# A float32 transformer trunk of split matmuls: the first blocks of x split straight from PSUM, and two column sets of the FFN's first projection taking turns

## The chip, the cores and the metric

The kernel runs on one core of a Trainium2 chip. The metric is the device time of one execution in microseconds; the times given are medians over runs of the same program. One profiled execution gives the trace.

## What is computed

The reference is a trunk of two layers on x (512 tokens by 1024 channels, float32). Each layer is an FFN, a token mixer (pooling, differential attention, a gated recurrence) and a second FFN, each with a norm ahead and a residual behind; a last norm ends it. The change touches the four FFNs only, whose first projection is this:

```
def swiglu(h, w_in, w_out):
    gate, up = jnp.split(h @ w_in, 2, axis=-1)
    return (jax.nn.silu(gate) * up) @ w_out
```

Here h is the normed x (512 x 1024) and w_in is 1024 x 5632, so gate and up have 2816 columns each.

## The kernel before

**Split matmuls.** Float32 values are split into a high and a low part (`wh` and `wl` of a weight block, `zh` and `zl` of the activations). One product is three matmuls: high by high, high by low, low by high. ScalarE makes the high part by a copy (`split_hi`), VectorE the low one by a subtraction (`low`, inside `split_hi`). A helper records every operation of the engines, so that nearly all rows have line 83, and operations are told apart by the names of their tiles.

**Seven products.** `seven()` computes a 2 x 2 block product by a scheme with seven block products, P1, P2, Q5, Q3, P6, P7, Q4, in this order. Their left operands are blocks of the transposed and gained x or sums of them: A11, A12, S1 (= A21 - A22), S4 (= A12 - S2), S2, S3, A22. Their right operands are sums of weight blocks, and these sums are not made by an engine: a block `raw` is loaded by SP's DMA queue (L368), used, and then changed in place by an accumulating DMA that GpSimd issues (L371) once the low part has been taken. The block b1 serves P1, Q5, P6 and Q4 in turn, b2 serves Q3 and P7. Each product has two units, n0 and n1, with a block of 256 rows each; a unit is 12 matmuls.

**Order of the work.** `ffn()` (L462) cuts the 2816 columns into six sets, `quad(j)` (L467): four of 512 columns and two of 384. Each set is 14 units, in the list `units`. The main loop runs a unit's matmuls and then `gap()`, which evicts what the unit completed and issues splits up to three units ahead:

```
for i in done:
    flush()
    ...
    u.after()
...
lows = splits_to(done[-1] + 3)
side.run()
```

Evictions are ScalarE copies (P1, Q5) and chains on VectorE: c (P2), v (Q3), and for P6 and P7 `u`, then `v` or `q5`; P6's six operations work on two row tiles. `defer(n, fn)` puts work n gaps later; `side` holds small work on parameters that runs in gaps with room. Loads are issued as far ahead as the number of blocks held (`held`, per set) allows. All blocks, high and low parts and most activations come from one pool of 43 tiles of 128 x 1024; PSUM has eight banks.

**The start.** `prologue` (L1271) loads parameters, constants and x on SP's queue, warms TensorE with matmuls on zeros, transposes a block of x into PSUM (`zt`), copies it to SBUF with the norm's gain (`zf`, ScalarE, four pieces of 256 columns), and splits it (`z_hilo`: `zh` by ScalarE, `zl` by VectorE, 1024 columns each). The four blocks of x follow each other (`z_block`), their sums for S1, S2, S3, S4 are made on VectorE (`zs`) and split, `squares` gathers the norm's sums of squares of x, and `derived_steps` computes parameters that the mixer needs, the first of them from a softplus of the recurrence's parameters (tiles `m`).

Of the kernel before, what the change touches and what calls it, by code (L numbers as in the profile page):

```python
# [9 lines left out]
F32R = mybir.dt.float32r  # L10
AF = mybir.ActivationFunctionType
ALU = mybir.AluOpType
ADD, SUB, MUL, MAX, MIN = ALU.add, ALU.subtract, ALU.mult, ALU.max, ALU.min
# [93 lines left out]
def trunk_kernel(ctx, tc, xn, pm, fin, cst, bd, f1i, f1o, win, wbp, wba, wbl, wout, f2i, f2o, out):  # L107
    nc = tc.nc
    V, A, PE, SP = Counted(nc.vector, 0.075, 0.00104), Counted(nc.scalar, 0.14, 0.00083), Counted(nc.tensor, 0.0, 0.00042), nc.sync
# [11 lines left out]
    def big(dt=F32, name="b"):  # L121
        return bp.tile([128, 2 * S], dt, tag="b", name=name)
# [8 lines left out]
    def bank(name="ps"):  # L131
        return pp.tile([128, S], F32, tag="ps", name=name)
# [4 lines left out]
    def f(t):  # L137
        return t.bitcast(F32)
# [3 lines left out]
    def flush():  # L142
        for fn in later:
            fn()
        later.clear()
# [13 lines left out]
    par = cp_.tile([128, NPAR], F32, tag="par", name="par")  # L159
# [18 lines left out]
    x = {}  # L178
    st = {"r": {}}
    units = []  # L180
# [7 lines left out]
    def defer(n, fn):  # L188

        tasks.setdefault(clock["gap"] + n, []).append(fn)  # L190
# [76 lines left out]
    def z_hilo(name):  # L267
        src = take(name)
        hi, lo = big(F32R, "zh"), big(F32R, "zl")
        A.activation(out=hi, in_=src, func=AF.Copy)  # L270
        later.append(lambda: V.tensor_tensor(out=lo, in0=src, in1=f(hi), op=SUB))
        zc[name] = (hi, lo)

    def z_sum(name, a, b, op):
        a, b = take(a), take(b)
        t = zf[name] = big(name="zs")
        V.tensor_tensor(out=t, in0=a, in1=b, op=op)

    def z_ready(role, n, got):

        got.add(role)
        if role == "A11":
            defer(n, lambda: z_hilo("A11"))
        if role in ("A21", "A22") and {"A21", "A22"} <= got:
            defer(n, lambda: (z_sum("S1", "A21", "A22", SUB), z_hilo("S1")))
            defer(n + 5, lambda: z_hilo("A22"))
        if role != "A12" and {"A11", "A21", "A22"} <= got:
            defer(n + 1, lambda: z_sum("S2", "S1", "A11", SUB))
            defer(n + 3, lambda: z_hilo("S2"))
            defer(n + 4, lambda: (z_sum("S3", "A11", "A21", SUB), z_hilo("S3")))  # L290
        if role == "A12":
            defer(n, lambda: z_hilo("A12"))
            defer(n + 1, lambda: (z_sum("S4", "A12", "S2", ADD), z_hilo("S4")))
            got.clear()
# [169 lines left out]
    def ffn(wi, wo, done, order0, rf, lim0=12):  # L464
        H = {}

        def quad(j, order, fresh):  # L467
            c0, w = ((0, 512), (16, 384), (4, 512), (19, 384), (8, 512), (12, 512))[j]
            u, c11, q5, v, th0, th1 = {}, {}, {}, {}, {}, {}
            held = {}  # L470

# [16 lines left out]
            def copies(dst):  # L488
                def fn(ps):
                    dst.update(enumerate(two("u")))  # L490
                    for tt in range(2):
                        A.activation(out=dst[tt][:, 0:w], in_=ps[tt][:, 0:w], func=AF.Copy)
                return fn
# [87 lines left out]
            def wap(r, c, k0, k1):  # L581
# [1 line left out]
                return wi[512 - r * 512 + k0 * 128:512 - r * 512 + k1 * 128, o:o + w].rearrange("(k p) f -> p k f", p=128)  # L583

            seven(order, 4, w, lambda name, k: [a[:, k * 256:k * 256 + 256] for a in zc[name]], wap,
                  {"P1": p1, "P2": p2, "Q5": copies(q5), "Q3": q3, "P6": p6, "P7": p7, "Q4": q4}, (lim0, 12, 10, 8, 8, 8)[j], fresh=fresh)

        n0 = len(units)
        later_order = ["P1", "P2", "Q5", "Q3", "P6", "P7", "Q4"]
        for j in range(6):  # L590
            quad(j, order0 if j == 0 else later_order, j == 0 and order0[1] == "Q5")
        nz = len(units) - 1
        add_hook(nz, zc.clear)

# [674 lines left out]


    def prologue(gain):  # L1271
        SP.dma_start(out=par, in_=pm)
        SP.dma_start(out=cs[:, 0:256], in_=cst[:, 0:256])
        warm = slot(F32R, "warm")
        V.memset(f(warm), 0.0)
        wps = bank("warm")

        def warming(n):
            for _ in range(n):
                PE.matmul(wps, lhsT=warm[:, 0:128], rhs=warm, start=True, stop=True)  # L1280

        warming(14)
        n = 0
        blocks_ = [(0, 1), (0, 0), (1, 0), (1, 1)]
        for hh, kk in blocks_:
            for tt in range(2):
                t = 2 * hh + tt
                x[t, kk] = slot(name="x")
                SP.dma_start(out=x[t, kk], in_=xn[t * 128:t * 128 + 128, kk * S:(kk + 1) * S])
            n = min(n + 2, 4)  # L1290
            loads(n)
        SP.dma_start(out=cs[:, 256:NCST], in_=cst[:, 256:NCST])
        roles = [role_of(hh, kk, 0) for hh, kk in blocks_]
        zb = [z_block(hh, kk, role, gain) for (hh, kk), role in zip(blocks_, roles)]
        zb[0]()
        warming(8)
        z_hilo("A11")
        flush()
        for fn in splits_to(0):
            fn()  # L1300
        zb[1]()
        lows = splits_to(1)
        z_hilo("A12")
        for fn in lows:
            fn()
        flush()
        for fn in splits_to(2):
            fn()
        defer(0, zb[2])
        defer(1, zb[3])  # L1310
        got = {"A11"}
        z_ready(roles[2], 1, got)
        z_ready(roles[3], 2, got)
        defer(4, lambda: (z_sum("S4", "A12", "S2", ADD), z_hilo("S4")))
        for i in range(4):
            defer(2 + i, lambda i=i: squares(i // 2, i % 2))
        side.gap += 1
        side.add("derived", derived_steps())

    def derived_steps():  # L1320
        def halves():
# [89 lines left out]
            state["dma"] += 1  # L1411
            state["held"] += len(b.loads)

    def split_hi(i):
        u = units[i]
        if not u.block:
            return lambda: None
        u.hi, u.lo = big(F32R, "wh"), big(F32R, "wl")
        todo = []
        for n, view, o, shape in u.pieces:  # L1420
            src = view(u.block.raw[n])
            size = math.prod(shape)
            cut = lambda t: t[:, o:o + size] if len(shape) == 1 else t[:, o:o + size].rearrange("p (k f) -> p k f", f=shape[-1])
            hi, lo = cut(u.hi), cut(u.lo)
            A.activation(out=hi, in_=src, func=AF.Copy)
            todo.append((lo, src, f(hi)))

        def low():
            for lo, src, hi in todo:
                V.tensor_tensor(out=lo, in0=src, in1=hi, op=SUB)  # L1430
            todo.clear()
            if u.acc:
                u.acc(u.block.raw[0])
            elif last_use[id(u.block)] == i:
                state["held"] -= len(u.block.raw)
                u.block.raw = None
            loads()
        return low

    def splits_to(i):  # L1440
        lows = []
        while state["split"] < len(units) and state["split"] <= i:
            lows.append(split_hi(state["split"]))
            state["split"] += 1
        return lows

# [131 lines left out]
```

## Time and profile before

| what | value |
|---|---|
| median of 3 runs | 2153.4 us (2152.71 to 2156.05) |
| profiled execution, its own time | 2148.72 us |
| its span | 2147.0 us |
| TensorE (PE) busy | 2086.4 us, 97% of the span |
| VectorE (DVE) busy | 1658.0 us, 77% |
| ScalarE (ACT) busy | 1192.8 us, 56% |
| data moved | 314.61 MB, mean 147 GB/s |

The busy times are shares of the whole span, which has stages of different kinds: the FFNs' first and second projections and the mixers. The four first projections are at the beginning of each FFN; the first starts the program. A wait in brackets behind a row is the idle time of that engine just before it, with the one that ended it. Matmul rows overlap: the distance between the starts of two of them is what one costs.

### The profile page before, as it was taken

The page shows a single profiled execution, that of the slowest core. Times are in us where ns is not written, and L with a number is a line of the kernel's source. Part 1 is how long each engine was busy: PE and PEld are TensorE (multiplying, and loading weights), DVE is VectorE, ACT ScalarE, POOL GpSimd, SP SyncE. Part 2 cuts the span into 40 slices and gives each one's busy share as a digit, 9 for nine tenths or more (in the row PEclk, how much of TensorE's full clock was granted, in tenths as well). Part 3 has the DMA queues.
Part 4 walks back from the last instruction along what each step waited for, and adds up shares of the span by engine and source line. Part 5 has one row for each costly group of instructions (what it writes and reads, how often), then busy time and mean ns, then how long its engine had stood idle before and what let it go on. Part 6 is the DMA issues. An engine that isn't in the chain of part 4 may idle for free. (4 is left out here: it accounts for less than half of the span.)

```text
span 2147.0 us, 26106 instructions
## 1 busy us (share of the span) xinstructions
PE 2086.4 (97%) x9648; PEld 1735.6 (81%) x9648; DVE 1658.0 (77%) x2355; ACT 1192.8 (56%) x1763; POOL 343.4 (16%) x292
## 2 busy tenths in 40 slices
PE   7999999999999999999999999999999999999998
PEld 5888888788787878987878988877887877888786
DVE  5877898598677487779977778976967766877797
ACT  6554565646563554546665555565455536555564
POOL 1222230000000022322312222300000000222230
PEclk9999999999999999999999999999999999999999
DMA  8888896122225278898967889941221353888894
GB/s 224 181 153 191 196 200 180 50 79 88 67 81 172 78 141 169 165 200 206 207 162 142 170 179 232 185 127 60 79 79 59 116 154 84 175 151 193 203 177 106
DMA packets 194096, 314.61 MB, mean 147 GB/s; under 512 B 10544, under 2 KB 86832, under 8 KB 193968
## 3 DMA queue, kind: packets, MB, share of 16 engines
q0 software_dynamic: 76288, 138.43, 38.9%
q1 hardware_dynamic: 117680, 174.51, 24.9%
q8 instruction: 75, 1.23, 0.2%
q14 instruction: 53, 0.43, 0.1%
HBM read 310.80 MB, written 2.10 MB: 146 GB/s over the span
## 5 line engine op out<-in xcount | busy, mean ns | idle before, releaser
L83 DVE TENSOR_TENSOR wl<-raw,wh 128x1024 fp32r<-128x1024 f32 (+2 forms) x696 | 709.1, 1038 | 204.6 <-ACT wh L83 202.4
L83 ACT ACTIVATE wh<-raw 128x1024 fp32r<-128x1024 f32 (+2 forms) x696 | 610.5, 906 | 264.5 <-DMA raw<-in_f1i_dram 115.4
L83 PE MATMUL ps<-z,wh 128*128 128x512 f32 x1216 | 380.1, 393 | 0.0
L371 POOL DMA_DIRECT2D raw<-in_f2i_dram x96 | 115.9, 1223 | 1133.5 <-DVE wl L83 390.1
L83 PE MATMUL P<-wl,zh 128*128 128x512 f32 (+1 forms) x768 | 287.5, 374 | 8.3 <-DVE wl L83 8.3
L83 PE MATMUL P<-wh,zh 128*128 128x512 f32 (+1 forms) x768 | 286.9, 374 | 2.1 <-ACT wh L83 2.1
L83 PE MATMUL P<-wh,zl 128*128 128x512 f32 (+1 forms) x768 | 285.9, 372 | 0.0
L83 PEld LDWEIGHTS ps<-z,wh 128*128 128x128 f32 x1216 | 227.1, 188 | 51.0 <-issue 3.4
L83 PE MATMUL ps<-z,wl 128*128 128x512 f32 x608 | 237.0, 390 | 0.0
L83 PE MATMUL Q<-wl,zh 128*128 128x512 f32 (+1 forms) x576 | 218.5, 379 | 14.5 <-DVE wl L83 14.5
L83 PE MATMUL Q<-wh,zh 128*128 128x512 f32 (+1 forms) x576 | 221.0, 384 | 7.5 <-ACT zh L83 3.9
L83 PE MATMUL Q<-wh,zl 128*128 128x512 f32 (+1 forms) x576 | 217.1, 377 | 5.4 <-DVE zl L83 5.4
L371 POOL DMA_DIRECT2D raw<-in_f1i_dram x96 | 116.0, 1232 | 377.8 <-DVE wl L83 276.5
L83 PEld LDWEIGHTS P<-wl,zh 128*128 128x128 f32 x768 | 144.5, 188 | 33.7 <-DVE wl L83 14.0
L83 PEld LDWEIGHTS P<-wh,zh 128*128 128x128 f32 x768 | 144.5, 188 | 24.3 <-ACT wh L83 4.4
L83 PEld LDWEIGHTS P<-wh,zl 128*128 128x128 f32 x768 | 144.6, 188 | 19.6
L83 PE MATMUL P<-wl,ah 128*128 128x512 f32 x352 | 138.2, 393 | 3.3 <-DVE wl L83 3.1
L83 PEld LDWEIGHTS Q<-wl,zh 128*128 128x128 f32 x576 | 109.6, 190 | 37.1 <-DVE wl L83 22.9
L83 PE MATMUL P<-wh,ah 128*128 128x512 f32 x352 | 137.4, 390 | 0.0
L83 PE MATMUL P<-wh,al 128*128 128x512 f32 x352 | 137.2, 390 | 0.0
L83 PEld LDWEIGHTS ps<-z,wl 128*128 128x128 f32 x608 | 114.1, 188 | 23.7
L83 PEld LDWEIGHTS Q<-wh,zh 128*128 128x128 f32 x576 | 109.8, 191 | 25.1 <-ACT zh L83 5.6
(189 smaller groups left out, 3412.2 us busy)
## 6 DMA issues: line engine op xcount, KB each, us to landing
raw<-in_win_dram SPq DMA_DIRECT2D x84, 512.0 KB, 4.3
raw<-in_f1i_dram POOLq DMA_DIRECT2D x64, 512.0 KB, 7.2
raw<-in_f2i_dram POOLq DMA_DIRECT2D x64, 512.0 KB, 6.9
raw<-in_f2i_dram SPq DMA_DIRECT2D x52, 512.0 KB, 5.1
raw<-in_f1i_dram SPq DMA_DIRECT2D x50, 512.0 KB, 5.8
raw<-in_f1o_dram POOLq DMA_DIRECT2D x40, 512.0 KB, 8.0
raw<-in_f2o_dram POOLq DMA_DIRECT2D x40, 512.0 KB, 8.2
raw<-in_f1o_dram SPq DMA_DIRECT2D x30, 512.0 KB, 7.3
```

Source lines behind the costliest of these rows:

```text
L83: return fn(*args, **kw)
L371: return lambda raw: GP.dma_start(out=raw[:, 0:n * w].rearrange("p (k f) -> p k f", f=w), in_=src, accum_op=ADD)
```

## The change

It has two parts, both in the order of work; what is multiplied with what stays the same.

In `ffn()`, the set (19,384) changes places with (4,512), so that both sets of 384 columns come second and third, and the 28 units of these two are put in turn: P1 of the one (two units), P1 of the other, P2 of the one, and so on. The number of blocks that may be held follows the sets.

```
-            c0, w = ((0, 512), (16, 384), (4, 512), (19, 384), (8, 512), (12, 512))[j]
+            c0, w = ((0, 512), (16, 384), (19, 384), (4, 512), (8, 512), (12, 512))[j]
...
-                  ..., (lim0, 12, 10, 8, 8, 8)[j], fresh=fresh)
+                  ..., (lim0, 12, 12, 10, 8, 8)[j], fresh=fresh)
...
         for j in range(6):
             quad(j, order0 if j == 0 else later_order, j == 0 and order0[1] == "Q5")
+            if j == 2:
+                n1 = len(units) - 28
+                units[n1:] = [units[n1 + 14 * s + 2 * p + n] for p in range(7) for s in range(2) for n in range(2)]
```

In `prologue`, the transfers of parameters and constants go to ScalarE's queue. A new `direct(b)` splits the blocks A11 and A12 of x straight from PSUM: ScalarE makes zh and VectorE zl, in four pieces each; the full copy zf, which the sums need, is made by ScalarE later (`full`). The first weight block's high part is made by VectorE, between the first and the second piece of zl. Eight warming matmuls behind the first transposes become six, the sums are deferred by fewer gaps, the squares by others, and the derived parameters by 30 gaps.

```
     def prologue(gain):
-        SP.dma_start(out=par, in_=pm)
-        SP.dma_start(out=cs[:, 0:256], in_=cst[:, 0:256])
...
+        nc.scalar.dma_start(out=cs[:, 0:256], in_=cst[:, 0:256])
+        nc.scalar.dma_start(out=par, in_=pm)
...
-        zb[0]()
-        warming(8)
-        z_hilo("A11")
-        flush()
-        for fn in splits_to(0):
-            fn()
-        zb[1]()
-        lows = splits_to(1)
-        z_hilo("A12")
...
+        def direct(b, mid=lambda: None):
+            (hh, kk), name = blocks_[b], roles[b]
+            hi, lo = zc[name] = (big(F32R, "zh"), big(F32R, "zl"))
+            ps = [bank("zt"), bank("zt")]
...
+            for m in range(4):
+                A.activation(out=cut(hi, m), in_=cut(ps[m // 2], m % 2), func=AF.Copy, scale=gain(4 * kk + m))
+            for m in range(4):
+                V.scalar_tensor_tensor(out=cut(lo, m), in0=cut(ps[m // 2], m % 2), scalar=gain(4 * kk + m), in1=f(cut(hi, m)), op0=MUL, op1=SUB)
+                if m == 0:
+                    mid()
+            def full():
+                t = zf[name] = big(name="zf")
+                uses[name] = 1
+                for m in range(4):
+                    A.activation(out=cut(t, m), in_=cut(ps[m // 2], m % 2), func=AF.Copy, scale=gain(4 * kk + m))
+            return full
+        def first():
+            for fn in splits_to(0, True):
+                fn()
+        full = direct(0, first)
+        warming(6)
+        lows = splits_to(1)
+        full()
+        for fn in lows + splits_to(2):
             fn()
...
+        defer(0, lambda: fulls.append(direct(1)))
+        defer(1, zb[2])
         defer(1, zb[3])
+        defer(2, lambda: fulls.pop()())
         got = {"A11"}
         z_ready(roles[2], 1, got)
-        z_ready(roles[3], 2, got)
-        defer(4, lambda: (z_sum("S4", "A12", "S2", ADD), z_hilo("S4")))
-        for i in range(4):
-            defer(2 + i, lambda i=i: squares(i // 2, i % 2))
+        z_ready(roles[3], 1, got)
+        defer(3, lambda: (z_sum("S4", "A12", "S2", ADD), z_hilo("S4")))
+        for i, k in enumerate((2, 3, 6, 7)):
+            defer(k, lambda i=i: squares(i // 2, i % 2))
         side.gap += 1
-        side.add("derived", derived_steps())
+        defer(30, lambda: side.add("derived", derived_steps()))
...
-            A.activation(out=hi, in_=src, func=AF.Copy)
+            if vector:
+                V.tensor_copy(out=hi, in_=src)
+            else:
+                A.activation(out=hi, in_=src, func=AF.Copy)
```

How this moves instructions is seen at three places.

VectorE in the first set, from the low weight part of unit 3 (P2, n1) on, where S1 is summed (`zs`) and split (`zl`). Before:

```order
L83 TENSOR_TENSOR wl<-raw,wh 128x1024
L83 TENSOR_TENSOR zs<-zf 128x1024
L83 TENSOR_SCALAR m<-m 128x8
L83 RECIPROCAL m<-m 128x8
L83 TENSOR_TENSOR m<-m 128x8 x2
L83 MEMSET m 128x8
L83 TENSOR_TENSOR zl<-zs,zh 128x1024
L83 TENSOR_TENSOR wl<-raw,wh 128x1024
L83 TENSOR_TENSOR zs<-zs,zf 128x1024
```

With the change:

```order
L83 TENSOR_TENSOR wl<-raw,wh 128x1024
L83 TENSOR_TENSOR zs<-zf 128x1024
L83 TENSOR_TENSOR zl<-zs,zh 128x1024
L83 TENSOR_TENSOR wl<-raw,wh 128x1024
L83 TENSOR_TENSOR zs<-zs,zf 128x1024
L83 TENSOR_TENSOR wl<-raw,wh 128x1024
L83 TENSOR_TENSOR zs<-zf,zs 128x1024
```

The four operations on m and the memset that stood between the sum and its split are gone from here; the sum for S4 (`zs<-zf,zs`) follows after one more weight part.

ScalarE over the same units, from the two evictions of P1 (`u`) to the weight part of unit 6 (Q3, n0). Before:

```order
L83 ACTIVATE u<-P_193 128x512
L83 ACTIVATE u<-P_194 128x512
L83 ACTIVATE zf<-zt,par 128x256 x4
L83 ACTIVATE wh<-raw 128x1024
L83 ACTIVATE zh<-zs 128x1024
L83 ACTIVATE q,m<-x 128x512 x2
L83 ACTIVATE wh<-raw 128x1024
L83 ACTIVATE m<-par 128x8
L83 ACTIVATE m<-m 128x8
L83 ACTIVATE q,m<-x 128x512 x2
L83 ACT_TABLE_LOAD
L83 ACTIVATE m<-m 128x2
L83 ACTIVATE wh<-raw 128x1024
```

With the change:

```order
L83 ACTIVATE u<-P_178 128x512
L83 ACTIVATE u<-P_179 128x512
L83 ACTIVATE zf<-zt,par 128x256 x8
L83 ACTIVATE zh<-zs 128x1024
L83 ACTIVATE wh<-raw 128x1024
L83 ACTIVATE zf<-zt,par 128x256 x4
L83 ACTIVATE q,m<-x 128x512 x2
L83 ACTIVATE wh<-raw 128x1024
L83 ACTIVATE zh<-zs 128x1024
L83 ACTIVATE q,m<-x 128x512 x2
L83 ACT_TABLE_LOAD
L83 ACTIVATE m<-m 128x2
L83 ACTIVATE wh<-raw 128x1024
```

Eight pieces of zf in one row, then four, stand where there were four and none; the two operations on m are gone, and zh of S4 stands ahead of the second squares and the table load.

VectorE in the second FFN, at the evictions of P6 in the first set of 384 columns. Before:

```order
L83 TENSOR_TENSOR wl<-raw,wh 128x768 x2
L83 TENSOR_TENSOR u<-P_6660,u 128x384
L83 TENSOR_TENSOR v<-v,u 128x384
L83 SCALAR_TENSOR_TENSOR v<-v,m,th 128x384
L83 TENSOR_TENSOR u<-P_6661,u 128x384
L83 TENSOR_TENSOR v<-v,u 128x384
L83 SCALAR_TENSOR_TENSOR v<-v,m,th 128x384
L83 TENSOR_TENSOR wl<-raw,wh 128x768 x2
L83 TENSOR_TENSOR u<-P_6704,u 128x384
L83 TENSOR_TENSOR u<-u 128x384
L83 TENSOR_TENSOR u<-P_6705,u 128x384
L83 TENSOR_TENSOR u<-u 128x384
```

With the change, where set A's P6 is followed by set B's:

```order
L83 TENSOR_TENSOR wl<-raw,wh 128x768 x2
L83 TENSOR_TENSOR u<-P_6833,u 128x384
L83 TENSOR_TENSOR v<-v,u 128x384
L83 SCALAR_TENSOR_TENSOR v<-v,m,th 128x384
L83 TENSOR_TENSOR u<-P_6834,u 128x384
L83 TENSOR_TENSOR v<-v,u 128x384
L83 SCALAR_TENSOR_TENSOR v<-v,m,th 128x384
L83 TENSOR_TENSOR wl<-raw,wh 128x768 x2
L83 TENSOR_TENSOR u<-P_6876,u 128x384
L83 TENSOR_TENSOR v<-v,u 128x384
```

Between one set's evictions of P6 and the next evictions stand two weight parts, as before, but the next evictions are those of the other set's P6, which are six operations and not four.

## Rows read from the trace of the kernel before

**Rows 1.** The page's first part: busy us of each engine, share of the span, instructions.
```profile
PE 2086.4 (97%) x9648; PEld 1735.6 (81%) x9648; DVE 1658.0 (77%) x2355; ACT 1192.8 (56%) x1763; POOL 343.4 (16%) x292
```

**Rows 2.** The waits: engine, line, for whom; us in total, times, longest.
```profile
PE Q L83 <- DVE wl L83: 16.0, 22, 1.9
```

**Rows 3.** TensorE's timeline of the start: start us, length, instruction, [idle before <-releaser].
```profile
6.25 1.03 PE L83 MATMUL zt<-cst,x 128*128 128x128 f32 x8
...
11.64 0.48 PE L83 MATMUL P<-wh,zh 128*128 128x512 f32 x1
...
30.50 0.79 PE L83 MATMUL Q<-wh,zl 128*128 128x512 f32 x1 [3.77 <-DVE zl L83]
...
34.93 0.60 PE L83 MATMUL Q<-wh,zh 128*128 128x512 f32 x1
...
45.27 0.53 PE L83 MATMUL Q<-wl,zh 128*128 128x512 f32 x1 [0.77 <-DVE wl L83]
...
49.60 0.49 PE L83 MATMUL P<-wh,zh 128*128 128x512 f32 x1
...
71.69 0.33 PE L83 MATMUL P<-wh,zh 128*128 128x384 f32 x1
```

**Rows 4.** Windows: span, PE, PEld, DVE, ACT, POOL busy; PEclk, DMA share, GB/s.
```profile
30.00:35.00 5.00, 4.50 (x11) 3.53 (x12) 4.83 (x13) 2.12 (x3) 1.20 (x1) 0.50 0.38 55
```

**Rows 5.** VectorE's timeline around the S1 block.
```profile
28.48 0.17 DVE L83 TENSOR_SCALAR m<-m 128x8 f32<-128x8 f32 x1 [3.63 <-ACT m L83]
```

**Rows 6.** ScalarE's timeline of the start.
```profile
6.89 1.57 ACT L83 ACTIVATE zf<-zt,par 128x256 f32<-128x256 f32 x4 [2.85 <-PE zt L83]
...
18.15 1.13 ACT L83 ACTIVATE u<-P 128x512 f32<-128x512 f32 x2
...
29.69 1.28 ACT L83 ACT_TABLE_LOAD   x1
```

**Rows 7.** Windows of the eight sets of 384 columns, columns as in rows 4.
```profile
71.69:105.57 33.88, 31.49 (x185) 30.78 (x184) 26.05 (x48) 18.14 (x28) 8.67 (x8) 1.00 0.81 156
145.27:177.21 31.94, 31.30 (x184) 30.65 (x182) 22.65 (x34) 16.93 (x26) 7.76 (x7) 1.00 0.86 173
787.20:822.19 34.99, 33.01 (x183) 31.85 (x182) 25.44 (x37) 17.75 (x26) 10.09 (x9) 0.95 0.75 138
861.90:892.96 31.06, 31.02 (x184) 30.62 (x183) 24.55 (x35) 17.78 (x26) 7.60 (x8) 1.00 0.86 172
1130.47:1164.76 34.29, 31.75 (x183) 30.53 (x182) 25.68 (x37) 17.64 (x26) 10.06 (x9) 1.00 0.77 142
1204.46:1235.80 31.34, 30.99 (x183) 30.60 (x182) 24.24 (x35) 17.67 (x26) 7.89 (x8) 1.00 0.84 171
1844.70:1877.61 32.91, 31.04 (x184) 30.63 (x182) 24.30 (x35) 17.97 (x26) 8.56 (x8) 1.00 0.80 147
1917.32:1948.53 31.21, 31.03 (x184) 30.64 (x182) 23.65 (x34) 17.60 (x26) 7.53 (x7) 1.00 0.87 171
```

**Rows 8.** Timeline of all engines in the third FFN's first 384-set; the page's DMA issues.
```profile
1153.82 0.84 ACT L83 ACTIVATE wh<-raw 128x768 fp32r<-128x768 f32 x1 [3.42 <-DMA raw<-in_f1i_dram]
...
1155.57 0.55 DVE L83 TENSOR_TENSOR u<-P,u 128x384 f32<-128x384 f32 x1
...
1159.00 1.82 DVE L83 TENSOR_TENSOR wl<-raw,wh 128x768 fp32r<-128x768 f32 x2
...
raw<-in_f1i_dram POOLq DMA_DIRECT2D x64, 512.0 KB, 7.2
```

**Rows 9.** VectorE by form: xcount | busy, mean ns of one | idle before, releaser.
```profile
L83 DVE TENSOR_TENSOR wl<-raw,wh 128x1024 fp32r<-128x1024 f32 x404 | 487.7, 1219 | 142.6 <-ACT wh L83 141.6
...
L83 DVE TENSOR_TENSOR wl<-raw,wh 128x768 fp32r<-128x768 f32 x112 | 105.8, 954 | 59.3 <-ACT wh L83 58.3 <-PE P L83 0.9
...
L83 DVE SCALAR_TENSOR_TENSOR z<-zt,par,z 128x512 fp32r<-128x512 f32 x16 | 11.1, 744 | 5.1 <-ACT z L83 4.9
...
L83 DVE TENSOR_SCALAR a<-a 128x512 f32<-128x512 f32 x8 | 3.4, 427 | 0.3
```

More of the change, by code (lines that the diff above doesn't have):

```diff
@@ L585, in quad @@
             seven(order, 4, w, lambda name, k: [a[:, k * 256:k * 256 + 256] for a in zc[name]], wap,
-                  {"P1": p1, "P2": p2, "Q5": copies(q5), "Q3": q3, "P6": p6, "P7": p7, "Q4": q4}, (lim0, 12, 10, 8, 8, 8)[j], fresh=fresh)
+                  {"P1": p1, "P2": p2, "Q5": copies(q5), "Q3": q3, "P6": p6, "P7": p7, "Q4": q4}, (lim0, 12, 12, 10, 8, 8)[j], fresh=fresh)
         n0 = len(units)
@@ L1294, in prologue @@
         zb = [z_block(hh, kk, role, gain) for (hh, kk), role in zip(blocks_, roles)]
-        zb[0]()
-        warming(8)
-        z_hilo("A11")
-        flush()
-        for fn in splits_to(0):
-            fn()
-        zb[1]()
-        lows = splits_to(1)
-        z_hilo("A12")
-        for fn in lows:
-            fn()
[L1306 to L1309, printed above, removed]
+        cut = lambda t, m: t[:, m * 256:m * 256 + 256]
+        def direct(b, mid=lambda: None):
[3 more added lines that the diff above has]
+            for m in range(4):
+                for tt in range(2):
+                    o = m % 2 * 256 + tt * 128
+                    PE.transpose(ps[m // 2][:, o:o + 128], x[2 * hh + tt, kk][:, m * 128:m * 128 + 128], ident)
+            for m in range(4):
[7 more added lines that the diff above has]
+                uses[name] = 1
+                for m in range(4):
+                    A.activation(out=cut(t, m), in_=cut(ps[m // 2], m % 2), func=AF.Copy, scale=gain(4 * kk + m))
+            return full
@@ L1310, in prologue @@
+        def first():
[6 more added lines that the diff above has]
+        for fn in lows + splits_to(2):
+            fn()
+        fulls = []
+        defer(0, lambda: fulls.append(direct(1)))
+        defer(1, zb[2])
         defer(1, zb[3])
+        defer(2, lambda: fulls.pop()())
         got = {"A11"}
         z_ready(roles[2], 1, got)
-        z_ready(roles[3], 2, got)
-        defer(4, lambda: (z_sum("S4", "A12", "S2", ADD), z_hilo("S4")))
@@ L1412, in loads, with split_hi @@
             state["held"] += len(b.loads)
-    def split_hi(i):
+    def split_hi(i, vector=False):
         u = units[i]
@@ L1438, in split_hi, with splits_to @@
         return low
-    def splits_to(i):
+    def splits_to(i, vector=False):
         lows = []
         while state["split"] < len(units) and state["split"] <= i:
-            lows.append(split_hi(state["split"]))
+            lows.append(split_hi(state["split"], vector))
             state["split"] += 1
```

## The prediction

> **What bounds the kernel now.** I read the page's head first: TensorE is busy 97% of the span and VectorE 77% [rows 1]. So a change to two short stretches can only give back TensorE's idle time there; no other engine is near enough to being the bound over the whole span. Second, the waits by engine: Q matmuls waited for the low weight parts (wl) of VectorE 22 times, 16.0 us in all, the longest 1.9 [rows 2]. Third, TensorE's timeline of the start [rows 3]: the first transposes at 6.25, the first product at 11.64, then one 128x512 matmul each 0.228 us (the page's 0.39 us of one overlap) until breaks come, two of them 3.77 us idle before 30.50 (zl, VectorE) and 0.77 before 45.27 (wl, VectorE). After the longer one, ten matmuls from 30.50 to 34.93 take 4.43 us instead of 2.28, and the granted clock of 30 to 35 us is 0.50 [rows 4], its 1.2 GHz level: about 2.0 us more than at 2.4 GHz, after 3.77 us of idling.
>
> Fourth, who was late at 30.50. VectorE's row at 28.48 waited 3.63 us for a tiny m of ScalarE [rows 5], which ScalarE had queued behind squares and a weight split; zl of S1 stands behind it in VectorE's order and ran only then. This m is the derived parameter work.
>
> Fifth, the eight sets of 384 columns [rows 7]. The second ones take 31.94 us in the first FFN and 31.06 to 31.34 in the others, nearly pure matmul, so 31.1 is the floor; the first ones take 33.88, 34.99, 34.29 and 32.91. Above the floor the eight have 12.8 us together. The rows of the third FFN say why [rows 8]: ScalarE waited 3.42 us for a block's accumulate (7.2 us from issue to landing), and VectorE with it; then the late wl and the six evictions of P6 (1155.57 to 1159.00, 3.43 us) met, and the next wl came only behind them. The waits of up to 1.9 us [rows 2] are of this kind.
>
> **The change, part by part.**
>
> *Start, up to unit 1.* Parameters and constants leave SP's queue, so x goes out two issues earlier. I cost that at 0: fourteen warming matmuls hold TensorE until 6.25, and the transposes there waited for nothing [rows 3]. If constants came late on the other queue, the transposes would start late by as much; 0.5 us is my bound. The Trainium skill, "DMA: Bandwidth & Descriptors", section "Issuing engines are not separate DMA queues", says that spreading issues over engines saves sequencer time and adds no bandwidth: by it the gain would be at most the time of two issues, by the row it is 0.
>
> From 6.25 on: four zh by ScalarE straight from PSUM end at 8.46 (the duration of the four zf now, 1.57 [rows 6]); VectorE makes zl0, about 0.42 (half of a 128x512 op of that form, 0.744 [rows 9]), then the first wh as a cast. No row shows a 1024-wide cast. Bounds: 0.70, twice less overhead the one-input op of 128x512 (0.427), and 1.22, the two-input op of 1024 columns. I take 0.70, since a cast has one input, and keep 0.5 us in the range. Then wl 1.22, which ends near 10.05; eleven matmuls at 0.228 end unit 0 at 12.6 (before: 11.64, two waits of 0.35, and ten by 0.228: 14.6). Unit 1 comes after eight transposes (0.9): 16.2. Sixteen transposes now stand before unit 2, eight of which are there now: unit 3 ends at 23.4 to 23.9.
>
> *Unit 4 (S1).* ScalarE: two u 1.13, eight zf 3.15 instead of four [rows 6], from 16.2 to 20.5; VectorE's sum 1.22 (as a wl [rows 9]); zh and wh about 1.0 each, zl and wl on VectorE some 1.15 apart (they overlap a little), and wl is there at 25.0, with no m in between since the derived work is deferred to gap 30. Unit 4 ends at 25.0 + 11 x 0.228 = 27.5 (before 34.93). **Gain 7.4**, the 3.77 and the 2.0 of slow matmuls being in it. The full copies are the cost: four ScalarE ops more per block (1.57 us), and 1.57 for two blocks lies on this path; that is in the sum.
>
> *Unit 6 (S4).* Here the saving is held up. Its sum now comes one gap earlier, but ScalarE has zf of the fourth block, two pairs of squares, one table load (1.28 [rows 6]) and an m ahead of or around wh6: by the rows' durations wh6 is done at 34.6, wl6 at 36.6. TensorE ended unit 5 at 31.2, so it idles 3.45 and 1.9 us with one or two matmuls between. That is idling like that before 30.50, so I charge the same 2.0 us for slow matmuls: unit 6 ends at 41.3, and of the 7.4 only 1.6 is left. The Trainium skill, "TensorE: Matmul & The Clock Gate", section "Part 1: The HAM clock gate (the "warmup" mystery)", says that an idle array is put back to 1.2 GHz and activity releases it; [rows 4] agree after 3.77 us. By it the 2.0 stand, without it the sum would be 11.9 instead of 11.1.
>
> *Units 7 to 13.* The wl of unit 7 comes at 40.7, the unit ends at 44.0 (before 49.5: from 45.27 it took 4.2 us for eleven matmuls, 1.6 more than by 0.228, which I do not expect again, since the wait shrinks below 0.5). Units 8 to 13 take 22.2 us now, with 16.4 of matmuls and 1.6 of transposes in them, so 4.2 of waits; the blocks of units 8 and 9 are ordered earlier against TensorE, which by my timeline takes 1.8 of those away, and units 10 to 13 keep theirs: 20.35. **The first set ends at 64.35 instead of 71.69: gain 7.3.**
>
> *The 384 sets.* Turns give an accumulate eight units (16.7 us) instead of four (8.4) against its 7.2, so the late blocks and VectorE's idle 3.31 vanish. What remains: P6's evictions of set A still take 3.43 us [rows 8] and stand, in VectorE's order, ahead of a wl. Counting from the end of P6A's last unit: wl .95, evictions until 4.35, next wl 5.25 where TensorE wants it at 4.35 (0.95 late), then after set B's evictions 10.45 against 10.07 (0.43 late), then no more. 1.4 us per FFN; in the first FFN the derived work (two dozen small ops and two table loads of 1.28) falls just there: 4.8. Against the losses now, (2.8+.8) (3.9+0) (3.2+.2) (1.8+.1), that is +1.2, -2.5, -2.0, -0.5: **-3.8**. A further price: two sets alive at once take more buffers, and four units per FFN get their wh and wl tiles only when the unit two before has ended (before: at least three, with a few exceptions). One unit is 2.08 us, the split 0.84 [rows 8] + 0.95 [rows 9] = 1.8: covered, by 0.3. I cost it at 0 and keep the rest for a rival.
>
> **Sum**: -7.3 - 3.8 = -11.1 us: 2148.7 of the profiled execution becomes 2137.6. The median of the three runs stands 4.7 higher, at 2153.4, so I forecast **2142.5**.
>
> **The rivals.**
>
> *B, ScalarE and the clock take the start's gain back* (0.20). If the slow level goes on through unit 7 (+2.4), the cast costs 1.22 and the transposes come 0.5 late, and if unit 8 is late by its accumulate, 5 to 7 of the 7.3 go; the total is then -4 to -6, at worst -1: about 2148. For it: the rows show slow matmuls twice in this stretch. Against it: in 30 to 35 us the DMA engines are busy only 0.38 of the time [rows 4], so the blocks of units 7 to 9 should not be what is late.
>
> *C, everything is covered* (0.10). Unit 6 gets its parts on time for a full clock, and the pair of sets loses nothing: -7.3 - 2 - 12.8 = -22, with half of it -16: 2131 to 2137. Against it: the burst of 3.43 us is in VectorE's order, whatever comes early.
>
> *D, slower through buffers* (0.08). If in those four units wl is begun only when the unit before has ended, each loses 0.84 + 0.95 = 1.8 us, 29 us over the four FFNs; less 12.8 and 7.3 it comes to +9: 2162. It decides from a lead of one unit; I count two, and ScalarE's copies (idle 3.42 now for want of data) would have to be behind by a whole unit. Against it: ScalarE is busy 18 us of 34 in these windows [rows 7].
>
> *E, the change does not do what it says* (0.07). The warmings hold the start, and the derived work is merely moved into the pair; the start then gives only what unit 4 gains, 2 to 3 us, and the pair 0 to 2: 2148 to 2151.
>
> **How the numbers follow.** The forecast as worked out has 0.55; its own range, with the cast's 0.5, the transposes' 0.5, and 2 us on either side for unit 6 and the pair, is 2138 to 2147. With B's better part and C the 8-in-10 range is 2134 to 2150. A measurement of this kernel tells about 0.2% (4.3 us) from nothing, so faster means under 2149.1. Faster: 0.55, 0.10 of C, and two thirds of B, 0.78 in all; same: the rest of B, E: 0.14; slower: D, 0.08.
>
> **What would show it.** In TensorE's timeline: first product near 9 instead of 11.64, unit 4 beginning its second matmul at 25 instead of 30.50, a break of some 3.5 us before unit 6 with slow spacing behind it, and the first 384-wide matmul at 64.4. In the windows of the pair: 63.6 to 64 us for both sets in FFNs two to four, 66 to 67 in the first, and no ScalarE idle time over 2 us that ends with the landing of raw. Wrong would be: a first 384-wide matmul after 68 (then B), pairs over 66 us with wh waiting for TensorE (then D), pairs of 62.2 (then C).

## The result, and the profile after

The changed kernel takes **2128.3 us** (4 runs, 2127.8 to 2129.4) against 2153.1 us (4 runs, 2150.9 to 2156.1) of the kernel before: a ratio of 0.9885, 95% interval 0.9868 to 0.9902, so 21 to 28 us faster. I had forecast 2142.5, with 2134 to 2150 as the range: the direction was right, the size (10.9 us) less than half of the measured 24.7. Measured again beside its parts on another chip, the ratio was 0.9913 (0.9900 to 0.9925), 19.7 us; the changed kernel itself came to 2128.1 to 2128.3 each time, the kernel before to 2146 to 2153.

The profiled execution fell from a span of 2147.0 to 2126.2 us. Of the page, the line that answers to [rows 1]:

```profile
PE 2079.0 (98%) x9646; PEld 1734.5 (82%) x9646; DVE 1660.1 (78%) x2362; ACT 1194.7 (56%) x1768; POOL 343.6 (16%) x292
```

VectorE, ScalarE and GpSimd are as busy as before; TensorE is so for 7.4 us less with the same matmuls (two warmings fewer), and the rest that went is its idle time. TensorE's timeline of the start, to be read against [rows 3]:

```profile
1.46 6.18 PE L83 MATMUL warm<-warm 128*128 128x512 f32 x14 [1.46 <-DVE warm L83]
7.47 1.03 PE L83 MATMUL zt<-cst,x 128*128 128x128 f32 x8
...
10.21 0.47 PE L83 MATMUL P<-wh,zh 128*128 128x512 f32 x1 [0.32 <-DVE wh L83]
...
26.13 0.50 PE L83 MATMUL Q<-wl,zh 128*128 128x512 f32 x1 [0.89 <-DVE wl L83]
...
35.47 0.80 PE L83 MATMUL Q<-wh,zh 128*128 128x512 f32 x1 [3.12 <-ACT wh L83]
...
37.59 0.79 PE L83 MATMUL Q<-wl,zh 128*128 128x512 f32 x1 [1.33 <-DVE wl L83]
...
65.26 0.33 PE L83 MATMUL P<-wh,zh 128*128 128x384 f32 x1
```

The windows of the changed kernel (columns as in [rows 4]): 35 to 40 us, then the pair of 384 sets of each of the four FFNs, against the eight windows of [rows 7]:

```profile
35.00:40.00 5.00, 3.20 (x7) 2.21 (x8) 4.78 (x11) 4.97 (x7) 1.20 (x1) 0.50 0.30 89
```

```profile
65.26:130.36 65.10, 61.54 (x359) 60.51 (x358) 50.58 (x101) 34.92 (x54) 19.21 (x16) 1.00 0.92 194
777.66:839.68 62.02, 61.10 (x357) 60.36 (x356) 48.44 (x72) 34.13 (x50) 20.56 (x17) 1.00 0.96 204
1116.80:1178.82 62.02, 61.07 (x358) 60.33 (x357) 48.12 (x71) 33.94 (x50) 20.23 (x17) 1.00 0.96 204
1826.56:1888.58 62.02, 61.10 (x357) 60.36 (x356) 47.67 (x70) 33.87 (x50) 19.32 (x16) 1.00 0.95 204
```

Three pairs agree to the hundredth; before, the same two sets took 64.1 to 66.1 us and no two FFNs alike. (The pair has eight transposes fewer in it, some 0.8 us, which the 512 sets behind it take over; so the sums below take both together.) Stage by stage, by the starts of the first matmul of each, the 20.8 us of the two spans are: the start until the first 384 set 6.4; the pairs with the three 512 sets behind them 9.5 (1.0, 3.8, 3.2, 1.4); the first sets of FFNs two to four 1.6; the second projections and the end 3.3. The mixers are the same to 0.1 us.

### The profile page after: what moved, and what is told of

Read it like the earlier page. It is cut to its first block, busy times and chain, and to the rows that moved or that the text cites. A ratio compares the mean times of both kernels' runs of the same rounds, so it can differ in the third digit from the quotient of the medians.

```text
span 2126.2 us, 26201 instructions
## 1 busy us (share of the span) xinstructions
PE 2079.0 (98%) x9646; PEld 1734.5 (82%) x9646; DVE 1660.1 (78%) x2362; ACT 1194.7 (56%) x1768; POOL 343.6 (16%) x292
## 4 chain that ended last, share of the span: by engine, by line
PE 78%; DVE 9%; issue 6%; ACT 4%; DMA 3%; POOL 0%; SPq 0%; DVEq 0%; POOLq 0%; ACTq 0%
PE P L83 27%; PE Q L83 20%; PE ps L83 18%; DVE wl L83 3%; PE y L83 3%; PE o L83 2%; PE ht L83 2%; PE v L83 2%; PE sc L83 1%; ACT wh L83 1%; DMA raw<-in_f1i_dram 1%; PE av L83 1%; DVE x L83 1%; DVE al L83 1%; DVE c L83 1%
## 5 line engine op out<-in xcount | busy, mean ns | idle before, releaser
L83 PEld LDWEIGHTS P<-wh,zl 128*128 128x128 f32 x768 | 144.2, 188 | 19.7
L83 PEld LDWEIGHTS Q<-wl,zh 128*128 128x128 f32 x576 | 109.2, 190 | 26.0 <-DVE wl L83 12.0
```

The costliest lines, as they stand in the source:

```text
L83: return fn(*args, **kw)
```

## The experiments

Sixteen runs were made, of twelve kernels, each beside the kernel before on the same chip. First, the two parts apart, and what the turns are made of.

**The start alone**: the sets, limits and their order as before.

```
-            c0, w = ((0, 512), (16, 384), (19, 384), (4, 512), (8, 512), (12, 512))[j]
+            c0, w = ((0, 512), (16, 384), (4, 512), (19, 384), (8, 512), (12, 512))[j]
...
-            if j == 2:
-                n1 = len(units) - 28
-                units[n1:] = ...
```

> The new start alone; the six column sets as before. The changed kernel gained 6.4 us up to its first 384-wide matmul by the profiles, and 24.7 us by the medians. Theory A (start and turns are separate gains; the rest comes from waits of the 384 sets): 6 to 8 us faster than before (2145 to 2147), first 384-wide matmul at 65 to 66 us, the first 384 set of each FFN still 33 to 35 us, and repeated executions still spread over some 5 us as the kernel before does. Rival B (the start sets off a chain that speeds the later stages too, so that the two parts only give 24.7 together): 12 us or more faster, with first 384 sets near 31.

Measured 2142.0 (12 runs, 2134.1 to 2149.3) against 2146.2 (19 runs, 2139.1 to 2153.3): ratio 0.9983 (0.9968 to 0.9999). Theory B falls. Theory A's way holds, with the first 384-wide matmul at 65.1, its figures do not: 4.3 us instead of 6 to 8, first 384 sets of 31.3 to 36.3 us, and runs over 15 us instead of 5. The four first 384 sets of its profile:

```profile
65.09:100.50 35.41, 32.92 (x183) 32.13 (x182) 25.58 (x36) 18.55 (x28) 10.27 (x9) 0.95 0.77 159
781.50:817.75 36.25, 33.52 (x184) 32.03 (x182) 26.87 (x39) 17.89 (x27) 11.51 (x10) 0.95 0.71 137
1127.95:1163.12 35.17, 32.86 (x183) 32.07 (x182) 26.46 (x38) 18.01 (x27) 11.47 (x10) 0.95 0.74 140
1844.11:1875.36 31.25, 30.99 (x184) 30.60 (x182) 23.21 (x35) 17.73 (x26) 8.55 (x8) 1.00 0.81 157
```

**The turns alone**: the kernel before with the part of the diff in `ffn()`.

```
+            c0, w = ((0, 512), (16, 384), (19, 384), (4, 512), (8, 512), (12, 512))[j]
...
+            if j == 2:
+                n1 = len(units) - 28
+                units[n1:] = ...
```

> The turns of the two 384 sets alone, with the start as before. Theory A: 14 to 19 us faster (2134 to 2139): pairs of 62.0 us in all four FFNs (the derived parameter work is at its old place, so the first FFN's pair has no wait either), the waits of the 512 sets and at the head of the second projections smaller by some 4 us in all, and repeated executions within 2 us of each other, because no wait depends on when an accumulate lands. My prediction's own sum says 3.8 to 7 us faster, since it takes 31.1 as the floor of a set; then pairs of 63.6 and over.

Measured 2132.6 (6 runs, 2128.7 to 2133.5), ratio 0.9940 (0.9924 to 0.9957): 13.6 us at the medians, just under theory A's 14 to 19 and clear of my sum's 3.8 to 7. Its first two pairs:

```profile
71.52:133.73 62.21, 61.25 (x359) 60.51 (x358) 49.11 (x83) 34.11 (x52) 19.23 (x16) 1.00 0.93 203
781.11:843.09 61.98, 61.03 (x358) 60.30 (x357) 47.73 (x71) 34.05 (x50) 19.82 (x17) 1.00 0.95 204
```

Here the derived work stands at its old place, and the first FFN's pair takes 62.2 instead of 65.1 us. Runs lie within 4.8 us of each other, not within 2 as expected; of the kernel before and of the start alone, which had more runs, within 14 and 15.

**Side by side without turns**: the changed kernel without the interleaving.

```
-            if j == 2:
-                n1 = len(units) - 28
-                units[n1:] = ...
```

> The changed kernel with the 384 sets side by side and the new limits of held blocks, but one after the other and not in turn. Theory A (an accumulate needs more than the four short units it has): the waits return in the first 384 set of each FFN and perhaps in the second, and the time is near the one with the new start alone, 2143 to 2149. Rival C (the order of the sets or the larger limit lets blocks come earlier, and the turns do little): within 4 us of the changed kernel, 2128 to 2132.

Measured 2152.0 (8 runs, 2146.1 to 2158.1), ratio 1.0034 (1.0017 to 1.0051), slower than before although it has the new start, and above theory A's 2143 to 2149 too. Its first two pairs:

```profile
65.35:136.80 71.45, 63.35 (x365) 61.12 (x364) 52.07 (x103) 35.38 (x56) 18.14 (x16) 1.00 0.80 168
788.46:857.09 68.63, 64.16 (x363) 62.32 (x362) 47.30 (x70) 34.05 (x52) 18.33 (x16) 0.98 0.81 169
```

The two sets took 66.9 to 71.5 us, and the granted clock is below 1.00 in three of the four pairs. Order and limits (rival C) give nothing by themselves, and side by side the two sets cost some 10 us more than apart; the turns give that back and more.

**Without the accumulates of the 384 sets**, one set after the other: the edit of the run just shown, and the sums of the weight blocks of these sets left out.

```
-                units.append(Unit(..., acc=acc, ...))
+                units.append(Unit(..., acc=None if width == 384 else acc, ...))
```

> The 384 sets one after the other as in the run without turns, and without the accumulating transfers of these two sets, so the sums of their weight blocks are left out and the output is another. If the accumulates' landing is what the 384 sets wait for: two sets of 62 to 63 us in all (without turns they took 67 to 71), 20 us faster than without turns, 2128 to 2132. If VectorE's evictions or buffers are what holds them: still 66 and more, 2140 to 2150.

Measured 2126.1 (4 runs), and the pairs of FFNs two to four at 62.9, 62.3 and 62.4 instead of 68.6, 70.6 and 66.9:

```profile
776.92:839.83 62.91, 61.94 (x363) 60.89 (x362) 50.23 (x74) 34.73 (x52) 0.38 (x1) 1.00 0.27 84
```

So it is mainly the accumulates that a 384 set waits for, not VectorE's evictions. The DMA share fell from 0.81 to 0.27 with them, so the run does not tell their landing from their traffic.

The 7.2 us of [rows 8] belong to the blocks of 512 KB, those of the 512 sets. The accumulates of the 384 sets are 384 KB each. Their rows, first for the first FFN's and third FFN's tensor over the whole trace, before and with turns, then for the second FFN before, at the last three accumulates of its first 384 set (issued from 801.5 to 807 us) and of its second (875 to 881):

```profile
raw<-in_f1i_dram POOLq DMA_DIRECT2D x32, 384.0 KB, 6.6
```

```profile
raw<-in_f1i_dram POOLq DMA_DIRECT2D x32, 384.0 KB, 7.2
```

```profile
raw<-in_f2i_dram POOLq DMA_DIRECT2D x3, 384.0 KB, 10.2
```

```profile
raw<-in_f2i_dram POOLq DMA_DIRECT2D x3, 384.0 KB, 6.8
```

So the turns don't make them faster, only earlier against their use. And it is not the median that a set waits for: four units are 8.4 us, and the last three accumulates took 8.3 to 10.2 us (medians of three) in the first sets of the four FFNs, 6.6 to 7.1 in the second ones. With turns the longest took 12.5 us, against 16.7. Why they take longer in the first sets of the kernel before is not shown.

**Derived parameters at 60 gaps instead of 30.**

```
-        defer(30, lambda: side.add("derived", derived_steps()))
+        defer(60, lambda: side.add("derived", derived_steps()))
```

> The changed kernel with the derived parameters put off by 60 gaps and not 30, into the 512 sets, where TensorE had no idle time at all. If the first FFN's pair (65.1 us against 62.0 in the others) is late only for them: its pair 62.0 and the whole 3 us faster, 2125. If its waits come of the first FFN's own transfers: pair still 64 to 65, no change (2128). If 512 sets can't hide the work either: pair 62, but the stretch behind it longer by 2 to 3 us.

Measured 2125.4 (6 runs, 2122.3 to 2128.1). The first FFN's pair, and the three 512 sets behind it:

```profile
64.26:126.24 61.98, 61.02 (x357) 60.28 (x356) 47.65 (x70) 34.23 (x51) 19.23 (x16) 1.00 0.94 204
126.24:246.79 120.55, 120.55 (x559) 100.12 (x559) 97.05 (x143) 66.16 (x85) 28.29 (x24) 1.00 0.83 179
```

The first expectation (62.0 and 2125): 3.1 us of the pair were the derived work, and the 512 sets hide it but for 0.4.

**Two tiles fewer in the large pool.**

```
-BIGS = 43
+BIGS = 41
```

> The changed kernel with 41 instead of 43 tiles in the large pool. It tries my rival of the buffers: in the pair ScalarE already starts a weight part only when the unit two before has ended. If that lead is spare: no change (within 1 us) and pairs of 62.0. If it is nearly used up: the pair's units wait 1 to 2 us each at P6 and P7, pairs of 66 to 70, and 8 to 29 us slower in all.

Measured 2164.2 (6 runs), 36 us over the changed kernel. The third FFN's pair and the sets behind it:

```profile
1136.74:1203.36 66.62, 63.17 (x357) 61.80 (x356) 46.83 (x69) 32.85 (x49) 18.82 (x16) 0.97 0.90 190
1203.36:1325.88 122.52, 120.80 (x557) 99.89 (x557) 93.52 (x113) 66.44 (x84) 29.01 (x24) 1.00 0.81 168
```

That is more than the expected 8 to 29. Fewer than two of the 43 tiles are spare. But half of it is not the pairs': by the profiles they lose 18.4 us (3.6 to 5.3 each), the 512 sets behind them 9.2 and the second projections 9.4. The kernel before was not run with 41 tiles, so how much of this the turns bring is not shown.

Then the start. **The changed kernel again**, as a yardstick:

> The changed kernel itself once more, as the yardstick for the others on this chip, since the kernel before came to 2153 in its first runs and to 2146 (19 runs) beside the last four kernels. If the change's gain is as first measured, 20 us or more below the kernel before again; if the two parts add (4.3 and 13.6 us by the medians), 16 to 20 us.

2128.1 (5 runs), ratio 0.9890 (0.9872 to 0.9909), 23.3 us: the first expectation on this chip.

**Unit 6's weight parts ahead of the squares** (one line added in the prologue):

```
+        defer(3, lambda: (later.extend(splits_to(6)), flush()))
```

> The changed kernel with the weight parts of unit 6 (Q3, n0) issued ahead of the second pair of squares, their table load and the m behind it. In the changed kernel TensorE idled 3.12 and 1.33 us around this unit and then ran at 1.2 GHz to 41.5. If ScalarE's order is what holds it: wh6 done near 32.7, wl6 near 34.2, no slow matmuls, unit 6 done 4 to 5 us earlier, and 3 to 5 us faster at the first 384-wide matmul (60.5 to 62 instead of 65.3). If the blocks of units 7 to 9 are the next bound: 1 to 2 us. If tanh and the gate come too late by this: a new wait at P6 (units 8, 9) and nothing gained.

Measured 2128.6: no gain. TensorE's waits over 0.8 us between 32 and 42 us, then ScalarE there:

```profile
33.19 0.50 PE L83 MATMUL Q<-wl,zh 128*128 128x512 f32 x1 [0.96 <-DVE wl L83]
...
39.02 0.62 PE L83 MATMUL Q<-wh,zh 128*128 128x512 f32 x1 [3.04 <-ACT wh L83]
```

```profile
35.40 1.28 ACT L83 ACT_TABLE_LOAD   x1
36.69 1.33 ACT L83 ACTIVATE th<-c,m 128x512 f32<-128x512 f32 x2
37.93 1.04 ACT L83 ACTIVATE wh<-raw 128x1024 fp32r<-128x1024 f32 x1
```

The 3 us moved from unit 6 to unit 7, whose weight part stands behind a table load and tanh: none of the three expected outcomes. ScalarE was without a break from 30 to 40 us.

**S4's sum, units 5 to 7 and tanh reordered.**

```
-        defer(3, lambda: (z_sum("S4", "A12", "S2", ADD), z_hilo("S4")))
-        for i, k in enumerate((2, 3, 6, 7)):
+        defer(2, lambda: (later.extend(splits_to(5)), z_sum("S4", "A12", "S2", ADD), z_hilo("S4")))
+        defer(3, lambda: (later.extend(splits_to(7)), flush()))
+        for i, k in enumerate((3, 3, 6, 7)):
...
-                defer(1, gate)
+                defer(3 if first else 1, gate)
```

> The changed kernel with S4's sum one gap earlier (ahead of the low part of unit 5), the weight parts of units 5, 6 and 7 ahead of all squares, and the first set's tanh two gaps later. Putting unit 6 alone ahead only moved the idle time of 3 us to unit 7, since ScalarE was busy throughout 30 to 40 us. If ScalarE's work between the sums and unit 8 is what is too much, and not its order: a wait of 3 us before unit 8 instead, and 0 to 1 us gained. If its idle 2.4 us ahead of zh of S4 and the tanh are what can be saved: 3 to 5 us at the first 384-wide matmul counted from the first product (50 to 52 instead of 55.1 us), and 2123 to 2125 in all.

From the first product to the first 384 set it took 54.2 instead of 55.1 us, 2126.3 in all: the first expectation by its numbers. The wait is now 2.1 us before unit 8; TensorE there, then ScalarE:

```profile
40.64 0.70 PE L83 MATMUL P<-wh,zh 128*128 128x512 f32 x1 [2.14 <-ACT wh L83]
```

```profile
38.59 1.06 ACT L83 ACTIVATE zh<-zs 128x1024 fp32r<-128x1024 f32 x1 [1.46 <-DVE zs L83]
39.55 1.04 ACT L83 ACTIVATE wh<-raw 128x1024 fp32r<-128x1024 f32 x1
```

Three orders came within 0.9 us of each other. That ScalarE's work alone is what is left does not follow: here it idled 1.46 us for a sum of VectorE's with unit 8's weight part queued behind. An order with that part ahead was not run.

**Ten warmings**, and, in a run of its own, **parameters on SP's queue again**:

```
-        warming(14)
+        warming(10)
```

```
     def prologue(gain):
+        SP.dma_start(out=par, in_=pm)
+        SP.dma_start(out=cs[:, 0:256], in_=cst[:, 0:256])
...
-        nc.scalar.dma_start(out=cs[:, 0:256], in_=cst[:, 0:256])
-        nc.scalar.dma_start(out=par, in_=pm)
```

> The changed kernel with 10 instead of 14 warming matmuls ahead of the first transposes. In the changed kernel they lasted to 7.47 us (at 0.43 us each for most of it), with x landed at 5.41 and the constants at 4.75. If they are what holds the start: transposes at 5.8, ScalarE's first zh at 7.0 (behind the parameters and a table load), first wl a microsecond earlier, 1 us faster in all. If the warmings are what brings the 2.4 GHz level: slow matmuls in unit 0, up to 2 us, which takes that back, no change or 1 us slower.

> The changed kernel with parameters and constants on SP's queue again, ahead of x. My sum has 0 for this part: the transposes start when the warmings end, x some 0.9 us later is still in time, no change within 1.5 us. If the start hangs on x: 0.9 us slower; if it hangs on the parameters (ScalarE's table load waited for them until 5.67): up to 1 us faster.

Ten: 2126.8, transposes at 5.89, and 55.1 from the first product on, as with fourteen: 1 us by the profile, inside the spread of the runs. SP's queue: 2126.8 (2126.1 to 2130.3), no change, as my sum had it, and as the Trainium skill, "DMA: Bandwidth & Descriptors", section "Issuing engines are not separate DMA queues", lets expect.

**All that helped together** (the new order, 60 gaps, ten warmings):

> All that helped in one kernel: the order of the start of the run beside it, derived parameters at 60 gaps, 10 warming matmuls. If these are separate: 3.1 (pair of the first FFN) and 0.8 (warmings) and what the new order gives, 2118 to 2122; at least 2125 if the order gives nothing.

2124.1 (4 runs, 2123.7 to 2125.7), between the two expectations. Its profile had 55.2 us from the first product to the first 384 set, a second profile of it, further down, 54.2, so the new order's 0.9 us does not always come.

At last the two parts, the whole and the best one on one chip, since the parts and the whole had been measured on different ones (us is the difference of the medians):

> The changed kernel, beside its two parts and the best version, all on one chip. If the two parts add, its gain over the kernel before is the sum of theirs within 3 us; if they need each other, it is 5 us or more above the sum (24.7 and 23.3 us were measured beside 4.3 and 13.6 on another chip).

> The new start alone again. If the gain up to the first 384-wide matmul is kept to the end: 5 to 8 us. If the derived work, which then falls into a 384 set without turns, takes some back: 3 to 5 us, with the first 384 set of the first FFN 1 to 2 us longer than the kernel before has it.

> The turns alone again. If what the turns give depends on how late accumulates land in the kernel before on this chip: the slower the kernel before here (2146 to 2153 so far), the larger the gain, 13 to 20 us, with the time itself again at 2131 to 2134.

> The best version again, now beside the changed kernel: 3 to 5 us faster than it (the first FFN's pair 62.0 instead of 65.1, and a start earlier by the warmings).

| kernel | median (runs) | ratio to before (interval) | us |
|---|---|---|---|
| before | 2147.8 (17) | | |
| start alone | 2141.7 (12) | 0.9978 (0.9966 to 0.9989) | -6.1 |
| turns alone | 2132.5 (5) | 0.9935 (0.9923 to 0.9946) | -15.3 |
| both: the change | 2128.2 (4) | 0.9913 (0.9900 to 0.9925) | -19.7 |
| best | 2123.8 (4) | 0.9891 (0.9878 to 0.9903) | -24.1 |

The parts add (21.4 against 19.7 by the medians; by the ratios 4.7 and 14.0 against 18.7). The best version's runs, 2122.1 to 2124.4, lie clear of the changed kernel's, 2126.6 to 2130.0. In this second execution of the start alone the same four first sets of 384, and the first FFN's second one, were:

```profile
64.40:95.51 31.11, 31.02 (x183) 30.62 (x182) 22.72 (x34) 17.46 (x27) 8.34 (x7) 1.00 0.89 181
779.52:813.26 33.74, 31.71 (x184) 30.50 (x182) 25.97 (x38) 17.75 (x26) 10.09 (x9) 1.00 0.78 145
1121.11:1156.74 35.63, 33.14 (x184) 32.07 (x182) 26.74 (x38) 18.13 (x27) 11.31 (x10) 0.95 0.73 141
1836.57:1867.67 31.10, 30.98 (x183) 30.60 (x182) 23.81 (x35) 17.99 (x26) 8.53 (x8) 1.00 0.83 157
138.79:169.48 30.69, 30.69 (x183) 30.62 (x182) 23.36 (x34) 17.62 (x26) 8.37 (x7) 1.00 0.86 174
```

The first took 35.41 in one execution and 31.11 in the other, of one kernel on two chips; the last line is a second set without any wait, 30.69. The derived work did not fall into a 384 set, as the expectation has it: in both profiles it ran in the 512 set behind (at 112 to 127 us here), and TensorE had no wait in that stretch.

## Why the prediction was wrong in size

Two terms of the sum failed: the 384 sets' -3.8, which measured -9.5 with the 512 sets behind them, and the 4.7 us added to get from the profile to the runs, which measured 0.4. Another 4.9 us came at places that the sum left out.

**The start: right, 0.9 short.** Forecast 64.35 for the first 384-wide matmul, measured 65.26 (alone 4.3 and 6.1 us at the medians of its two runs). Unit by unit it went as worked out, later by 0.9 to 1.3 us up to there: the first wl used at 11.4 (10.05), unit 4's at 26.1 (25.0), unit 6 from 35.5 with wl at 37.6 (34.6 and 36.6). The idle 3.12 and 1.33 us had been 3.45 and 1.9. Slow matmuls followed, granted clock 0.50 in 35 to 40 us, as charged. The Trainium skill, "TensorE: Matmul & The Clock Gate", section "Part 1: The HAM clock gate (the "warmup" mystery)", whose rule on an idle array I had weighed there, agrees with that row. The lateness is the step "fourteen warming matmuls hold TensorE until 6.25": the same fourteen held it until 7.47 here, and in the run at 60 gaps, where they held it until 6.46, the first 384-wide matmul came at 64.26. From the first product on, twelve profiles of kernels with this start (one with unit 6 ahead) give 55.05 to 55.13 us.

**The turns: right in mechanism, the size wrong.** What remained in a pair was as forecast: 0.95 us late behind P6A's evictions, measured 0.90, and 0.43 behind P6B's, measured about 0.3; VectorE's and TensorE's rows of the third FFN, beside [rows 8]:

```profile
1156.11 0.55 DVE L83 TENSOR_TENSOR u<-P,u 128x384 f32<-128x384 f32 x1
...
1159.54 1.82 DVE L83 TENSOR_TENSOR wl<-raw,wh 128x768 fp32r<-128x768 f32 x2
```

```profile
1160.55 0.44 PE L83 MATMUL P<-wl,zh 128*128 128x384 f32 x1 [0.90 <-DVE wl L83]
```

The evictions still take 3.43 us. Wrong was the step "so 31.1 is the floor" with "above the floor the eight have 12.8 us together", and -3.8 came of it. A set without a wait takes 30.7. The "floor" had waits in it, too short for a bracket: in the set of 31.06 two matmuls stand 0.38 and 0.28 us apart, the others around them 0.17:

```profile
887.80 0.34 PE L83 MATMUL Q<-wh,zh 128*128 128x384 f32 x1
888.18 0.45 PE L83 MATMUL Q<-wl,zh 128*128 128x384 f32 x1
888.46 0.34 PE L83 MATMUL Q<-wh,zl 128*128 128x384 f32 x1
```

Against 30.7 the eight windows of [rows 7] hold 16.1 us of waits and slow matmuls, not 12.8. And a pair has fewer transposes than two sets apart: by counting `ht` in the windows, 28 stood in the two sets, 20 in the pair, since those of both Q4 come behind it. So what I had at 63.6, two floors and 1.4, is 62.02: two sets of 30.69, less some 0.85 for eight transposes, and 1.5 lost at the two places by the spacing there. In FFNs two to four the 512 sets give back 0.2 to 0.7 us.

Two smaller readings in this term were wrong too. The derived work was put at 3.4 us more (4.8 against 1.4) and cost 3.1; but "two table loads of 1.28" were in it, and ScalarE's trace has no table load between 64.2 and 330 us, so the nearness is chance. And "against its 7.2" took the row of the 512 KB blocks: by a median of 6.6 to 7.2 against 8.4 no 384 set would wait at all. It is the late ones that wait.

**Not in the sum**: 1.6 us at first sets and 3.3 at the second projections. I can't put these on the turns: the start alone, which has none, had second projections of 108.3, 110.6 and 109.7 us in its first profile, where the kernel before had 109.2, 111.0 and 109.5. Accumulates may be what they wait for too: in 755 to 775 us of the trace of before, four of them had a median of 8.4 us, against 6.9 for that tensor over the whole page. That is argued from single executions, and stays open.

**From the profile to the runs.** The step "the median of the three runs stands 4.7 higher, at 2153.4, so I forecast 2142.5" carried the 4.7 over to the changed kernel. It does not have them: its profiled execution and its median differ by 0.4. The standard deviation of the kernel before was 2.8 to 4.4 us in the four sessions with 9 to 19 runs of it, that of the start alone and of the one without turns 2.6 to 4.6 (8 to 12 runs), that of all kernels with turns and 43 tiles 0.7 to 2.2 (4 to 6 runs). Between two executions of the start alone, the first 384 sets differed by up to 4.3 us: by this the waits that the turns take away are drawn anew in each execution, and the one profiled was short for its chip (2148.7 beside 2150.9 to 2156.1).

Together, as profiles: 20.8 measured, 11.1 forecast; 5.7 of the difference are pairs and 512 sets, 4.9 what was not in the sum, less 0.9 of the start. The rest, up to the medians' 24.7, I put on the spread.

**The rivals.** C came nearest in size (2131 to 2137) and not by its way: unit 6 was late and the clock fell, and its "burst of 3.43 us" stayed. By my sign "pairs of 62.2 (then C)" it came, but that sign was built on the 31.1; the pairs still lose 1.5 us. B did not come. Of E both conditions held in part, the warmings until 7.47 and the derived work in the pair, yet the start gave 6.4 us up to the first 384 set and not 2 to 3. D, the slower one, needs two tiles fewer, and then 3.6 to 5.3 us a pair, not the 7.2 of its sum.

## What to carry to other kernels

Where a wait ends with the landing of a transfer, one trace shows one draw of it: compare the runs' spread and the same stage in several places, look at the late landings and not at the median, and at the row with the size of the stage in question. Take as floor a stretch that shows no wait at all, by the spacing of its matmuls, not the shortest at hand. Here, doubling the work between a transfer's issue and its use gave more than the waits of one trace, and the spread shrank with it; how many buffers are spare for it is worth one run of its own. Moving work ahead on an engine that has no idle time in the stretch only moves the wait.

## Not expected

The fourteen warming matmuls, identical in all these kernels, ended between 6.1 and 7.5 us, since they are 0.43 us apart at first and 0.23 later, and the change of pace came at another time in each execution, between the seventh and the fourteenth of them (4.2 and 7.2 us); I found no queue and no landing that goes with it. The granted clock is given as 1.00 all the while (the window of 2 to 3 us of the changed kernel):

```profile
2.00:3.00 1.00, 1.00 (x4) 0.75 (x3) 0.00 (x0) 0.00 (x0) 0.00 (x0) 1.00 0.82 185
```

But these fourteen took 6.01 us, from 1.46 to 7.47, 0.43 each, about the pace of the ten from 30.50 to 34.93 of before (4.43 us, [rows 3]), where the granted clock was 0.50 [rows 4], its 1.2 GHz level. So at a program's start the spacing has to be read, not that column. (The x4 in the line counts the matmuls that touch the window, and they overlap.) The Trainium skill, "TensorE: Matmul & The Clock Gate", section "Part 1: The HAM clock gate (the "warmup" mystery)", says that the number of slow matmuls at a start varies from run to run; the traces agree, with six to thirteen here.

The cast of 1024 columns by VectorE, for which no row stood, took 0.68 us; 0.70 had been taken for it. A subtraction of that size takes 1.22.
